# A hybrid residual block on one core: the second projection's product order, the place of its operand steps, and the start of the depthwise convolution's accumulators

## The chip, the cores and the metric

The kernel runs on one core of one Trainium2 chip. The metric is the device time of one execution in microseconds (us), the median over runs. The unchanged kernel was run three times; a fourth execution was recorded by the hardware profiler, and every row of the trace comes from that one.

## What is computed

One layer of a streaming encoder, on 1024 positions with 1024 channels. Two mixers share one input projection, and their outputs are gated, added and projected again; a feed-forward part follows.

```
proj = h @ w_in                       # h = adaLN(rmsnorm(x), c)
b, c, v, v_c, gl_c, gates = split(proj)
y_a = (b * causal_dwconv3(c * v)) @ w_short_out
u   = causal_dwconv31(v_c * sigmoid(gl_c)) + conv_conf_b
y_b = silu(layer_norm(u)) @ w_conf_out
g_a, g_b = split(sigmoid(gates))
x = x + g1 * ((g_a * y_a + g_b * y_b) @ w_o)
x = x + g2 * ((silu(h2 @ wa) * (h2 @ wb)) @ w_ffn_out)   # h2 = adaLN(rmsnorm(x), c)
return rmsnorm(x)
```

The shift, scale and gate vectors of adaLN (`sh1 ... g2`) come from `silu(c) @ w_ada + b_ada`, 48 blocks of 128 values.

## The kernel before

**Layout.** Channels lie on the 128 partitions, in 8 blocks; positions lie along the free dimension in two halves of 512. All matrix products are fp32 with both factors split into a high and a low part, so that a product of two 128x128 by 128x512 pieces takes three matmuls: high by high (L504), low activation by high weight (L505), high activation by low weight (L507). ScalarE (ACT) makes the high parts by a cast, of a weight at L243 (`wh`) and of an activation at L544 (for the second projection `z1h`, `z2h` and so on); VectorE (DVE) makes the low parts by a subtraction (L244, L545), for the weights of most of the input projection GpSimd (POOL).

**Seven products.** A pair of 1024x1024 weight quarters is multiplied by a scheme of the Strassen and Winograd kind: seven products, named "1" to "7", of 24 matmuls each (two output blocks `p`, four blocks `k` of 128 channels, three matmuls) in place of eight. Some products need sums of weight quarters and sums of activations first. `product` (L516) takes the next split weight from `next_w` (L465), which keeps the weights of the two following products in preparation (`AHEAD` = 2), and then issues the matmuls into PSUM banks `x`, `y`, `z`; `evac` takes the results out.

**The stages in order of time.** Start and norm; the input projection `w_duals` (some 100 to 560 us), beside which DVE runs the depthwise convolution of width 31; the first mixer's projection `w_short` ("ya"); the second mixer's projection `w_conf` ("yb", some 635 to 715 us), which this case calls the second projection; the output projection `w_o` ("mix"); the feed-forward part.

**Who orders the work.** The program text gives an order, and a scheduler lays out each engine's queue from it, at times in another order; each engine then takes its queue in the order laid out, and an instruction whose inputs are not there holds what stands behind it. `tc.issue_after(ins)` asks the scheduler to place the enclosed instructions behind `ins`.

**The second projection.** Two halves `d` of output channels have seven products each, 14 in all; `CONF_ORDER` (L120) and `yb_order` (L459) set their order, before 1(0) 1(1) 2(0) 2(1) 5(0) 5(1) 6(0) 6(1) 7(0) 7(1) 4(0) 4(1) 3(0) 3(1), where the bracket holds `d`. The weights come from `conf_units` (L384): SP loads a quarter (`get`, L390), and where a sum is needed POOL issues a second transfer that adds another quarter on the way (`add`, L397). Product 5 takes quarter 22 with 21 added; product 6 adds quarter 11 to that on DVE (L407, the tile `s2`); product 7 takes 21 with 11 added; product 3 adds quarter 12 onto product 6's own tile (L411), so this transfer waits until product 6's split has read the tile. `s2(0)` is `raw_5431` and `s2(1)` is `raw_5482` in the queues below. The activations' sums and splits for the coming products are called by `z_steps` (L1429) behind a product: `z_5`, `z_6`, `z_7`, `z_4` and `z_3`, each for four blocks `k`. `yb_evac` (L1376) copies a bank out on ACT (`vz`, L1395), or multiplies it by a gate on DVE and adds the result to `ma` by an adding transfer that POOL issues (L1388). The gates `gb` are loaded by POOL as well (`gates_b`, L1415), into six buffers that come free as those adding transfers land. So POOL's queue in this stage holds three kinds of transfers one behind the other: gate loads, adding transfers into `ma`, and adding transfers into weight tiles.

**The convolution.** `conv(j)` (L1143) runs once for each of 8 channel blocks. It works on even and odd positions apart, with two accumulators `a0` and `a1` in PSUM (the names `c0` and `c1` in the trace): 15 taps on the odd positions `od`, a sum, and 15 and 16 taps on differences (`diff`). A tap is one DVE instruction (L1158). The two accumulators are begun on ACT, `a0` with tap 1 and the bias (L1165), `a1` with tap 2 (L1166), and the odd taps go to `a0`, the even ones to `a1`. The results go to `cv` in DRAM and into running sums `tot` on POOL.

**The modulations.** In the input projection, seven pairs of product steps ("5" and "3" of `d` 3 to 9) each also compute one of the 48 adaLN blocks: a 128x1024 block of `w_ada` is loaded by SP into a free weight buffer, and DVE reduces it (L485). L1254 to L1256 do this after the product's call.

Of the kernel before, what the change touches and what calls it, by code (L numbers as in the profile page):

```python
# [37 lines left out]
AF = mybir.ActivationFunctionType  # L38
ALU = mybir.AluOpType
# [77 lines left out]
PRODUCTS = "1265734"  # L117


CONF_ORDER = "1256743"  # L120


MOD_FROM, MOD_AT = 16, "53"
# [15 lines left out]
def block_kernel(ctx: ExitStack, tc: tile.TileContext, x0, xT, c, vecs, ada, w_first, w_plain, w_duals,  # L139
# [69 lines left out]
    def col(base, k):  # L209
        return vec[:, base + k : base + k + 1]  # L210
# [245 lines left out]
    ya_order = [(d, m) for m in "12" for d in range(2)] + [(d, m) for d in range(2) for m in PRODUCTS[2:]]  # L456
    ya_units = [added_units([w_short[d, m] for m in range(4)]) for d in range(2)]
    plan += [ya_units[d][m] for d, m in ya_order]
    yb_order = [(d, m) for m in CONF_ORDER for d in range(2)]  # L459
    yb_units = [conf_units([w_conf[d, m] for m in range(4)], d) for d in range(2)]  # L460
    plan += [yb_units[d][m] for d, m in yb_order]
    plan += [(w_o[k], 1024) for ks in (range(KC), SECOND[KEPT:]) for k in ks]
# [680 lines left out]
    def conv(j):  # L1143
        eo = u[j].rearrange("p (n two) -> p n two", two=2)
        ev, od = eo[:, :, 0], eo[:, :, 1]
        diff = diffp.tile([P, T + CK - 1], F32, tag="diff", name="diff")
        d, e = diff[:, :NE], diff[:, NE : 2 * NE - 1]
        with tc.issue_after(read_at(conv_at(j))):
            nc.vector.tensor_tensor(d, ev, od, ALU.subtract)
            nc.vector.tensor_tensor(e, ev[:, 1:], od[:, : NE - 1], ALU.subtract)  # L1150
        a0, a1 = ps2_tile("c0"), ps2_tile("c1")
        n = 0

        def tap(out, src, s, wt, acc):
            nonlocal n
            n += 1
            with tc.issue_after(read_at(conv_at(j + n / TAPS))):
                tap.ins = nc.vector.scalar_tensor_tensor(  # L1158
                    out=out, in0=src[:, s : s + H], scalar=wt, in1=acc, op0=ALU.mult, op1=ALU.add
                ).ins  # L1160

        def both(s):
            return col(V_CW + 2 * s * KC, j) if s == CK // 2 else wsum[:, s * KC + j : s * KC + j + 1]

        nc.scalar.activation(a0, od[:, 1 : 1 + H], AF.Identity, bias=col(V_CB, j), scale=both(1))  # L1165
        nc.scalar.activation(a1, od[:, 2 : 2 + H], AF.Copy, scale=both(2))  # L1166
        for s in range(3, CK // 2 + 1):
            acc = a0 if s % 2 else a1
            tap(acc, od, s, both(s), acc)
        tap(od[:, :H], od, 0, both(0), a1)  # L1170
        with tc.issue_after(tap.ins):
            nc.vector.tensor_tensor(a0, a0, od[:, :H], ALU.add)
        for s in range(CK // 2):
            tap(eo[:, :H, 1] if s == CK // 2 - 1 else a1, e, s, col(V_CW + (2 * s + 1) * KC, j), a1 if s else a0)
        for s in range(CK // 2 + 1):
            tap(eo[:, :H, 0] if s == CK // 2 else a0, d, s, col(V_CW + 2 * s * KC, j), a0)
# [54 lines left out]
    for d, m in win_order:  # L1231
# [8 lines left out]
        if d + 1 < BEGUN and m == PRODUCTS[-1]:  # L1240
            for p in range(2):
                nc.scalar.copy(win_banks[d + 1]["x", p], m1[2 * (d + 1) + p])
        with tc.issue_after(mm3.ins) if (d, m) == (0, "6") else ExitStack():
            product(win_banks[d], m, th[m], win_evacs[d], onto="2")
        if (d, m) == win_order[0]:
# [5 lines left out]
                nc.gpsimd.memset(tot[h], 0.0)  # L1251
        if win_order.index((d, m)) >= len(win_order) - 7:
            q_steps.pop(0)()
        if m in MOD_AT and BEGUN < d < GATED:  # L1254
            modulation_of(MOD_FROM + n_mod, load(ada[MOD_FROM + n_mod], home=dual_units.home))
            n_mod += 1  # L1256
    while late:
        late.pop(0)()
# [167 lines left out]
    def z_3(k):  # L1426
# [2 lines left out]
    z_steps = {  # L1429
        (0, "1"): each(z_first, 4, 5), (1, "1"): each(z_first, 6, 7),  # L1430
        (0, "2"): each(z_5, 0, 1), (1, "2"): each(z_5, 2, 3), (0, "5"): each(z_6, 0, 1), (1, "5"): each(z_6, 2, 3),
        (0, "6"): each(z_7, *range(KH)), (1, "6"): each(z_4, *range(KH)), (1, "7"): each(z_3, *range(KH)),
        (0, "4"): lambda: [mg_split(j, 0) for j in range(0, KC, 2)],
    }
    for d, m in yb_order:
# [554 lines left out]
```

## Time and profile before

| | |
|---|---|
| median of 3 runs | 1456.21 us (1456.04 to 1456.32) |
| the profiled execution's own time | 1457.19 us |
| span of its trace | 1455.4 us |
| mean granted clock of TensorE | 0.995 |
| busy, share of the span | PE 99%, PE weight loads 81%, DVE 83%, ACT 45%, POOL 36% |
| DMA | 275.04 MB, mean 189 GB/s |

The span is what the trace covers from first to last instruction; the execution's own time is 1.8 us longer, for what lies around it. All times in the trace count from the span's start. PE is TensorE, SP the engine that issues most loads. In a row of the timeline stand the start, the length, the engine, the line and operation, output and inputs with their shape, the count of merged instructions, and in square brackets how long the engine had been idle before and what ended that. The matmuls' ends are modelled, and a matmul of 0.39 us stands next to the following one at a distance of 0.227 us, since they overlap.

### The profile page before, as it was taken

To read this page: it belongs to the slowest core of one execution; us is meant where nothing else is said; L and a number is where in the kernel's file an instruction comes from. 1 tells how busy PE (TensorE), PEld (TensorE's weight loads), DVE (VectorE), ACT (ScalarE), POOL (GpSimd) and SP (SyncE) were. 2 spreads that over 40 slices of the span, in tenths; PEclk is the share of its full clock that TensorE was granted. 3 is DMA by queue.
4 is the path that set the end of the run, shared out by engine and by line. 5 is a ranking of instruction groups with operands and counts; after the bars stand their busy time and mean duration, and the time that the engine had idled before them with its cause. 6 is when DMAs were issued, how large, how long until landed. Compare 5 with 4: busy or idle time off the path is not lost.

```text
span 1455.4 us, 17728 instructions
## 1 busy us (share of the span) xinstructions
PE 1434.4 (99%) x6322; PEld 1177.1 (81%) x6322; DVE 1204.0 (83%) x1657; ACT 656.6 (45%) x963; POOL 522.2 (36%) x496
## 2 busy tenths in 40 slices
PE   8999999999999999998999999999999999999997
PEld 4888888788878888887888888888888888888887
DVE  7996999999998998988988798877777665866676
ACT  4873433333333456566535464444444443322235
POOL 0016787677766661012222001101111115653405
PEclk9999999999999999999999999999999999999999
DMA  9743223333335569867795437645555449995903
GB/s 344 282 159 95 65 97 121 102 116 102 131 130 180 162 214 322 219 198 180 200 342 170 142 103 261 212 162 166 170 176 177 141 141 361 391 384 173 352 0 116
DMA packets 95946, 275.04 MB, mean 189 GB/s; under 512 B 10945, under 2 KB 12993, under 8 KB 95858
## 3 DMA queue, kind: packets, MB, share of 16 engines
q1 hardware_dynamic: 46672, 148.92, 30.1%
q0 software_dynamic: 44000, 111.36, 25.5%
q10 hardware_dynamic: 5186, 13.64, 2.4%
q8 instruction: 49, 0.80, 0.2%
q14 instruction: 39, 0.32, 0.1%
HBM read 203.09 MB, written 67.63 MB: 186 GB/s over the span
## 4 chain that ended last, share of the span: by engine, by line
PE 51%; POOL 1%; issue 0%; DVE 0%; POOLq 0%
PE x L507 8%; PE x L505 8%; PE x L504 8%; PE z L505 4%; PE z L507 4%; PE z L504 4%; PE y L504 2%; PE y L507 2%; PE y L505 2%; PE mix L504 2%; PE mix L507 2%; PE mix L505 2%; POOL x L1873 1%; PE bank L505 1%; PE bank L504 1%; PE bank L507 1%
## 5 line engine op out<-in xcount | busy, mean ns | idle before, releaser
L243 ACT CAST wh<-raw 128x1024 fp32r<-128x1024 f32 (+2 forms) x254 | 262.8, 1036 | 384.1 <-PE bank L505 137.6
L244 DVE TENSOR_TENSOR wl<-raw,wh 128x1024 fp32r<-128x1024 f32 (+2 forms) x176 | 211.7, 1204 | 42.1 <-ACT wh L243 40.2
L244 POOL TENSOR_TENSOR wl<-raw,wh 128x1024 fp32r<-128x1024 f32 x78 | 195.8, 2513 | 108.5 <-ACT wh L243 108.5
L1158 DVE SCALAR_TENSOR_TENSOR c<-diff,vec,c 128x512 f32<-128x512 f32 x232 | 165.0, 748 | 1.4
L1628 POOL DMA_DIRECT2D hid<-stage x70 | 37.4, 535 | 343.9 <-DVE stage L553 322.1
L504 PE MATMUL bank<-th,wh 128*128 128x512 f32 x336 | 132.1, 393 | 3.0 <-DVE sc L857 3.0
L505 PE MATMUL bank<-tl,wh 128*128 128x512 f32 x336 | 131.8, 392 | 0.0
L507 PE MATMUL bank<-th,wl 128*128 128x512 f32 x336 | 131.7, 392 | 0.0
L504 PEld LDWEIGHTS bank<-th,wh 128*128 128x128 f32 x336 | 63.7, 190 | 16.7 <-DVE sc L857 3.4
L505 PEld LDWEIGHTS bank<-tl,wh 128*128 128x128 f32 x336 | 63.8, 190 | 13.4
L507 PEld LDWEIGHTS bank<-th,wl 128*128 128x128 f32 x336 | 63.8, 190 | 13.3
L552 ACT CAST stage<-g 128x512 fp32r<-128x512 f32 x60 | 37.3, 621 | 76.9 <-DMA hid<-stage 41.0
L1158 DVE SCALAR_TENSOR_TENSOR c<-u,wsum,c 128x512 f32<-128x512 f32 x96 | 70.0, 747 | 0.8 <-ACT c L1166 0.2
L505 PE MATMUL x<-tl,wh 128*128 128x512 f32 x176 | 68.5, 389 | 0.0
L504 PE MATMUL x<-th,wh 128*128 128x512 f32 x176 | 68.5, 389 | 0.0
L507 PE MATMUL x<-th,wl 128*128 128x512 f32 x176 | 68.4, 390 | 0.0
L553 DVE TENSOR_TENSOR stage<-g,stage 128x512 fp32r<-128x512 f32 x60 | 41.2, 689 | 29.3 <-ACT stage L552 29.1
L1652 POOL DMA_DIRECT2D th<-hid x77 | 41.1, 534 | 51.4 <-PE x L507 33.9
L485 DVE CUSTOM_DVE_ANT_0 raw<-raw,cs,vec 128x1024 f32<-128x1024 f32 x24 | 40.1, 1670 | 12.3 <-DMA raw<-in_ada 12.3
L264 DVE TENSOR_TENSOR raw<-raw 128x1024 f32<-128x1024 f32 (+1 forms) x15 | 17.8, 1188 | 37.2 <-DMA raw<-in_w_fi 26.1
L1652 POOL DMA_DIRECT2D tl<-hid x77 | 41.2, 535 | 19.5 <-PE x L507 4.1
L504 PE MATMUL bank<-t2h,wh 128*128 128x512 f32 x112 | 43.6, 389 | 0.0
(830 smaller groups left out, 4149.4 us busy)
## 6 DMA issues: line engine op xcount, KB each, us to landing
hid<-stage POOLq DMA_DIRECT2D x70, 512.0 KB, 4.8
raw<-in_w_duals SPq DMA_DIRECT2D x65, 512.0 KB, 3.7
raw<-in_w_fi SPq DMA_DIRECT2D x54, 512.0 KB, 4.5
th<-hid POOLq DMA_DIRECT2D x77, 256.0 KB, 5.8
tl<-hid POOLq DMA_DIRECT2D x77, 256.0 KB, 5.9
ada<-in_ada SPq DMA_DIRECT2D x24, 512.0 KB, 7.1
raw<-in_ada SPq DMA_DIRECT2D x24, 512.0 KB, 3.6
raw<-in_w_fo SPq DMA_DIRECT2D x16, 512.0 KB, 6.1
```

The costliest lines, as they stand in the source:

```text
L243: hi = nc.scalar.copy(wh, raw)
L244: lo = lo_engine.tensor_tensor(wl, raw, f32(wh), ALU.subtract)
L264: eng.tensor_tensor(a["s1"], a["21"], a["22"], ALU.add)
L485: nc.vector.tensor_tensor_reduce(out=raw, in0=raw, in1=cs, scale=1.0, scalar=col(V_ADA, b), op0=ALU.mult, op1=ALU.add, accum_out=modc(b),)
L504: nc.tensor.matmul(ps, wh, xh, start=first, stop=False, skip_group_check=again)
L505: nc.tensor.matmul(ps, wh, xl, start=False, stop=False, skip_group_check=again)
L507: mm3.ins = nc.tensor.matmul(ps, wl, xh, start=False, stop=last, skip_group_check=again).ins
L552: t_split.act = nc.scalar.copy(hi, src).ins
L553: t_split.ins = nc.vector.tensor_tensor(lo, src, f32(hi), ALU.subtract).ins
L1158: tap.ins = nc.vector.scalar_tensor_tensor(out=out, in0=src[:, s : s + H], scalar=wt, in1=acc, op0=ALU.mult, op1=ALU.add).ins
L1628: nc.gpsimd.dma_start(hid_dram[key], s)
L1652: nc.gpsimd.dma_start(t, hid_dram[key][:, s])
```

## The change

Three edits.

**The order of the second projection.** `CONF_ORDER` now lists pairs: 1(0) 1(1) 2(0) 2(1) 5(0) 5(1) 6(0) 6(1) 3(0) 7(0) 7(1) 4(0) 4(1) 3(1). Product 3(0) has moved from the 13th place to the 9th. The operand steps follow: behind 6(0) now stand all of `z_3` (before `z_7`), behind 6(1) `z_7` (before `z_4`), and behind 3(0) `z_4` (before, `z_3` stood behind 7(1)). Since the weights are prepared two products ahead, the weight of 3(0) is now prepared while 6(0) is computed.

**The convolution.** `a0` is begun on DVE by a `tensor_scalar`; taps 2 to 5 all go to `a0`; `a1` is begun on ACT with tap 6, placed behind the last of these; taps 7 to 15 alternate as before. Each of the 8 convolutions has one instruction fewer on ACT and one more on DVE.

**The modulations.** The load of the `w_ada` block is now issued before the product's call, and the reduction is wrapped in `issue_after(mm3.ins)`, the last matmul of that product.

```diff
-CONF_ORDER = "1256743"
+CONF_ORDER = [(d, m) for m in "1256" for d in range(2)] + [(0, "3")] + [(d, m) for m in "74" for d in range(2)] + [(1, "3")]
...
-    yb_order = [(d, m) for m in CONF_ORDER for d in range(2)]
+    yb_order = CONF_ORDER
...
-        nc.scalar.activation(a0, od[:, 1 : 1 + H], AF.Identity, bias=col(V_CB, j), scale=both(1))
-        nc.scalar.activation(a1, od[:, 2 : 2 + H], AF.Copy, scale=both(2))
-        for s in range(3, CK // 2 + 1):
+        with tc.issue_after(read_at(conv_at(j))):
+            nc.vector.tensor_scalar(a0, od[:, 1 : 1 + H], both(1), col(V_CB, j), ALU.mult, ALU.add)
+        for s in (2, 3, 4, 5):
+            tap(a0, od, s, both(s), a0)
+        with tc.issue_after(tap.ins):
+            nc.scalar.activation(a1, od[:, 6 : 6 + H], AF.Copy, scale=both(6))
+        for s in range(7, CK // 2 + 1):
             acc = a0 if s % 2 else a1
             tap(acc, od, s, both(s), acc)
...
+        mod_raw = load(ada[MOD_FROM + n_mod], home=dual_units.home) if m in MOD_AT and BEGUN < d < GATED else None
         with tc.issue_after(mm3.ins) if (d, m) == (0, "6") else ExitStack():
             product(win_banks[d], m, th[m], win_evacs[d], onto="2")
...
-        if m in MOD_AT and BEGUN < d < GATED:
-            modulation_of(MOD_FROM + n_mod, load(ada[MOD_FROM + n_mod], home=dual_units.home))
+        if mod_raw is not None:
+            with tc.issue_after(mm3.ins):
+                modulation_of(MOD_FROM + n_mod, mod_raw)
             n_mod += 1
...
-        (0, "6"): each(z_7, *range(KH)), (1, "6"): each(z_4, *range(KH)), (1, "7"): each(z_3, *range(KH)),
+        (0, "6"): each(z_3, *range(KH)), (1, "6"): each(z_7, *range(KH)), (0, "3"): each(z_4, *range(KH)),
```

What the scheduler makes of it is seen in the queues. A row there gives the line, the operation, the output and its inputs with their tile numbers, the shape, and in brackets the semaphores on which the instruction waits: `DMASW` stands for a transfer that POOL issued, `DMAHW` for one that SP issued, the other names for engines.

ACT's queue at the time of products 5(1) and 6(0), before. `wh_5536` is the high weight of product 7(0), made from `raw_5533`, which an adding transfer of POOL fills:

```order
L243 CAST wh_5485<-raw_5482 128x1024 [waits DVE_49,Activation_49]
L544 CAST z6h_5470<-t2z_5468 128x512 [waits DVE_49]
L1269 ACTIVATE cv7_4987<-cv7_4987,vec_95 128x512 [waits DVE_49]
L243 CAST wh_5536<-raw_5533 128x1024 [waits DMASW2_49,PE_49,Activation_49]
L544 CAST z6h_5478<-t2z_5476 128x512 [waits DVE_49]
L1395 COPY vz_5501<-y_5279 128x512
L1395 COPY vz_5515<-y_5280 128x512 [waits PE_49]
L544 CAST z6h_5521<-t2z_5519 128x512 [waits DVE_49]
L544 CAST z6h_5529<-t2z_5527 128x512 [waits DVE_49]
```

The same place now. `wh_5534` is the high weight of product 3(0), made from `raw_5431`, which is `s2(0)` with quarter 12 added:

```order
L243 CAST wh_5485<-raw_5482 128x1024 [waits DVE_49,Activation_49]
L544 CAST z6h_5470<-t2z_5468 128x512 [waits DVE_49]
L1275 ACTIVATE cv7_4987<-cv7_4987,vec_95 128x512 [waits DVE_49]
L243 CAST wh_5534<-raw_5431 128x1024 [waits DMASW3_49,PE_49,Activation_49]
L544 CAST z6h_5478<-t2z_5476 128x512 [waits DVE_49]
L1401 COPY vz_5501<-y_5279 128x512
L1401 COPY vz_5515<-y_5280 128x512 [waits PE_49]
L544 CAST z6h_5521<-t2z_5519 128x512 [waits DVE_49]
L544 CAST z6h_5529<-t2z_5527 128x512 [waits DVE_49]
```

One row has changed: between the first two blocks of product 6's activations that are cast here now stands the weight of 3(0), not that of 7(0), and it waits for another transfer of POOL. PE's queue, the same before and now, takes these blocks so (`bank_829` and `bank_830` belong to 6(0), `bank_831` to 6(1)):

```order
L504 MATMUL bank_829<-z6h_5470,wh_5434 128x512 [waits Activation_49]
L504 MATMUL bank_830<-z6h_5470,wh_5434 128x512
L505 MATMUL bank_829<-z6l_5471,wh_5434 128x512 [waits DVE_49]
L507 MATMUL bank_829<-z6h_5470,wl_5435 128x512
L505 MATMUL bank_830<-z6l_5471,wh_5434 128x512
L507 MATMUL bank_830<-z6h_5470,wl_5435 128x512
L504 MATMUL bank_831<-z6h_5470,wh_5485 128x512
L505 MATMUL bank_831<-z6l_5471,wh_5485 128x512
L504 MATMUL bank_829<-z6h_5478,wh_5434 128x512 [waits Activation_49]
```

Eight matmuls use the block `z6h_5470`; the ninth is the first that needs `z6h_5478`.

POOL's queue in the same stage, before. `raw_5431` and `raw_5588` are the weights of 3(0) and 7(1), `ma40` and `ma60` take the results of product 2(1):

```order
L397 DMA raw_5533<-in_w_conf 128x1024 [waits DMAHW1_49,DMASW2_49,DVE_49]
L1388 DMA ma00_4669<-gb_5325 128x512 [waits DMASW3_49,DVE_49]
L1388 DMA ma20_4683<-gb_5327 128x512 [waits DMASW4_49,DVE_49]
L1415 DMA gb_5645<-gate_b3_121 128x512 [waits DMASW5_49,DMASW3_49]
L1415 DMA gb_5683<-gate_b5_123 128x512 [waits DMASW6_49,DMASW4_49]
L1388 DMA ma40_4731<-gb_5378 128x512 [waits DMASW7_49,DVE_49]
L1388 DMA ma60_4745<-gb_5380 128x512 [waits DMASW0_49,DVE_49]
L1415 DMA gb_5685<-gate_b7_125 128x512 [waits DMASW7_49,DMASW1_49]
L1415 DMA gb_5739<-gate_b1_119 128x512 [waits DMASW2_49,DMASW0_49]
L397 DMA raw_5431<-in_w_conf 128x1024 [waits DVE_49]
L397 DMA raw_5588<-in_w_conf 128x1024 [waits DMAHW2_49]
```

And now; `raw_5582` and `raw_5641` are the weights of 7(0) and 7(1):

```order
L397 DMA raw_5582<-in_w_conf 128x1024 [waits DMAHW1_49,DMASW2_49,DVE_49]
L1394 DMA ma00_4669<-gb_5325 128x512 [waits DMASW3_49,DVE_49]
L1394 DMA ma20_4683<-gb_5327 128x512 [waits DMASW4_49,DVE_49]
L1421 DMA gb_5639<-gate_b2_120 128x512 [waits DMASW5_49,DMASW3_49]
L1421 DMA gb_5698<-gate_b1_119 128x512 [waits DMASW6_49,DMASW4_49]
L1394 DMA ma40_4731<-gb_5378 128x512 [waits DMASW7_49,DVE_49]
L1394 DMA ma60_4745<-gb_5380 128x512 [waits DMASW0_49,DVE_49]
L1421 DMA gb_5700<-gate_b3_121 128x512 [waits DMASW7_49,DMASW1_49]
L1421 DMA gb_5738<-gate_b5_123 128x512 [waits DMASW2_49,DMASW0_49]
L397 DMA raw_5431<-in_w_conf 128x1024 [waits DVE_49]
L397 DMA raw_5641<-in_w_conf 128x1024 [waits DMAHW2_49]
```

The gates are those of other products, but the kinds of transfers stand in the same order: the addition for 3(0) stands behind two gate loads, and these wait for the landing of `ma40` (`DMASW7`) and `ma60` (`DMASW0`).

ACT's queue in the convolution stage, in the fourth convolution, before:

```order
L952 ACTIVATE bank_830<-bank_830 128x512 [waits PE_49]
L922 COPY bank_827<-bank_831 128x512 [waits DVE_49,PE_49]
L1165 ACTIVATE c0_4256<-u3_1605,vec_95,wsum_109 128x512 [waits DVE_49]
L922 COPY bank_828<-bank_832 128x512 [waits PE_49]
L854 ACTIVATE bank_829<-p3_1834,vec_95 128x512
```

And now:

```order
L952 ACTIVATE bank_830<-bank_830 128x512 [waits PE_49]
L922 COPY bank_827<-bank_831 128x512 [waits DVE_49,PE_49]
L243 CAST wh_2064<-raw_1962 128x1024 [waits PE_49,Activation_49]
L922 COPY bank_828<-bank_832 128x512 [waits DVE_49,PE_49]
L854 ACTIVATE bank_829<-p3_1834,vec_95 128x512 [waits DVE_49]
```

The begin of the accumulator between the two copies of banks is gone from ACT, and a cast of a weight has come into its place. On DVE the two reductions of one `d` now stand close together in every `d`. Around the last pair (`raw_3115` and `raw_3187`, where `raw_2974` and `raw_3148` stood) the rows have the same sequence as before: reduction, two taps, four instructions of the short convolution (L857), a sum (L869), one L857, reduction, L857. The single reduction that stood alone behind it (of `raw_3229`) is gone, and one more now stands at the stage's begin.

## The prediction

> **What bounds the kernel now.** I read the page's busy times first, then PE's waits, then the queues at the two longest waits.
>
> ```profile
> PE 1434.4 (99%) x6322; PEld 1177.1 (81%) x6322; DVE 1204.0 (83%) x1657; ACT 656.6 (45%) x963; POOL 522.2 (36%) x496
> PE bank L504 <- ACT z7h L544: 3.7, 1, 3.7
> PE bank L504 <- DVE sc L857: 3.0, 1, 3.0
> ...
> PE bank L504 <- ACT bank L922: 1.1, 1, 1.1
> ```
>
> PE is busy 99% of the span, and the matmuls are the same before and after. So the time can change only at PE's gaps, at the clock behind a gap, and by new gaps. Three gaps lie where the change acts: 3.7 us in the second projection, 3.0 and 1.1 us in the input projection. The rows left out belong to the kernel's start, which is untouched. The gap in the second projection costs more than its length:
>
> ```profile
> 687.10 0.39 PE L504 MATMUL bank<-z7h,wh 128*128 128x512 f32 x1
> 691.19 0.50 PE L504 MATMUL bank<-z7h,wh 128*128 128x512 f32 x1 [3.70 <-ACT z7h L544]
> ...
> 691.10:695.60 4.50, 4.41 (x12) 3.13 (x13) 3.72 (x5) 4.03 (x8) 0.00 (x0) 0.62 0.54 137
> 695.60:700.00 4.40, 4.40 (x21) 3.64 (x20) 3.29 (x6) 2.33 (x4) 0.83 (x1) 1.00 0.32 111
> ```
>
> The first two rows are the timeline of PE; in the others stand the stretch, the busy time and count of PE, weight loads, DVE, ACT and POOL, then the granted clock. Behind the gap the clock is 0.62 for 4.5 us, so 1.7 us are lost there: this gap costs 3.7 + 1.7 = 5.4 us. Its cause is named `z7h`, but the timeline of ACT shows what held that cast:
>
> ```profile
> 675.33 1.05 ACT L243 CAST wh<-raw 128x1024 fp32r<-128x1024 f32 x1 [0.54 <-ACT cv L1269]
> 676.29 0.61 ACT L544 CAST z6h<-t2z 128x512 fp32r<-128x512 f32 x1
> ...
> 685.11 0.64 ACT L544 CAST z7h<-cv 128x512 fp32r<-128x512 f32 x1
> 689.57 1.04 ACT L243 CAST wh<-raw 128x1024 fp32r<-128x1024 f32 x1 [3.83 <-DMA raw<-in_w_conf]
> 690.52 0.61 ACT L544 CAST z7h<-cv 128x512 fp32r<-128x512 f32 x1
> ```
>
> The next block's `z7h` stood behind the cast of 7(1)'s weight, which waited 3.83 us for an adding transfer. From the start of that cast, which begins when the transfer has landed, to PE's resumption (691.19) passed 1.6 us. So a weight cast that waits for POOL's transfer stops PE if an activation cast that PE needs stands behind it.
>
> **The change part by part: the second projection.** At the place of the row at 675.33, where ACT cast 7(0)'s weight without waiting for it, now stands the cast of 3(0)'s weight, and behind it the `z6h` of the row at 676.29. When does 3(0)'s transfer land? One row of DVE, one of SP, then POOL's timeline and landing times:
>
> ```profile
> 670.05 1.22 DVE L244 TENSOR_TENSOR wl<-raw,wh 128x1024 fp32r<-128x1024 f32 x1
> ...
> 668.40 9.70 SPq L227 DMA_DIRECT2D raw<-in_w_conf  x3
> ...
> 668.47 1.85 POOL L1388 DMA_DIRECT2D ma<-gb  x2
> 676.32 0.57 POOL L1415 DMA_DIRECT2D gb<-gate_b  x1 [6.00 <-DMA ma<-gb]
> 677.96 0.56 POOL L1415 DMA_DIRECT2D gb<-gate_b  x1 [1.07 <-DMA ma<-gb]
> 678.51 1.84 POOL L397 DMA_DIRECT2D raw<-in_w_conf  x2
> ...
> DMA to landing us min/median/max: 7.3/8.0/8.6
> DMA to landing us min/median/max: 5.2/7.9/12.4
> DMA to landing us min/median/max: 8.1/8.1/8.1
> ```
>
> The landings are of the two `ma` transfers at 668.47, of all six adding transfers for weights, and of the first at 678.51. POOL stood at two gate loads until the `ma` transfers had landed, and issued 3(0)'s addition at 678.51, though its tile had been free since product 6(0)'s low part was made, at 670.05 + 1.22 = 671.3. Before, this had no price, since 3(0) came 13th. Now the same two waits stand ahead of it in POOL's queue, and the products 2(0) and 2(1) that they follow from are unmoved. So the issue stays at 678.5, and the landing lies between 678.5 + 5.2 = 683.7 and 678.5 + 8.1 = 686.6. I take 684.8, between the ends: the last of SP's three loads (issued near 678 before, for product 4(1)) now has to wait for 3(0)'s own tile, and leaves this stretch less crowded.
> ```profile
> 675.31 0.62 PE L504 MATMUL bank<-z6h,wh 128*128 128x512 f32 x2
> ...
> DMA to landing us min/median/max: 3.2/4.6/8.6
> ...
> L244 DVE TENSOR_TENSOR wl<-raw,wh 128x1024 fp32r<-128x1024 f32 (+2 forms) x176 | 211.7, 1204 | 42.1 <-ACT wh L243 40.2
> ```
>
> An outer bound: the second row is that of the adding transfers into `ma` from 655 to 700 us. If those two landed near the least and the middle of these, after 3.2 to 4.6 us, the gate loads would go at 673 to 674, 3(0)'s addition near 674.5, and it would land near 680.
>
> PE begins product 6 at 675.31. In the new queue eight matmuls use the block cast before that point, at 0.227 us each, so PE stops near 677.1. It resumes 1.6 us behind the landing: 684.8 + 1.6 = 686.4. The gap is 9.3 us (8.2 to 11.1; 4.5 for the outer bound). Behind it the clock falls as it did behind the gap of 3.7 us and of 3.0 us:
>
> ```profile
> 427.00:430.00 3.00, 0.02 (x1) 0.00 (x0) 3.00 (x4) 1.77 (x3) 2.84 (x2) 0.87 0.12 19
> 430.00:436.00 6.00, 5.99 (x14) 4.74 (x15) 5.83 (x10) 1.05 (x2) 1.62 (x2) 0.50 0.96 336
> 436.00:440.00 4.00, 4.00 (x18) 3.25 (x18) 4.00 (x5) 2.22 (x4) 2.30 (x1) 0.99 0.02 8
> ```
>
> At 430 the clock was 0.50 for about 5.7 us, so some 2.8 us were lost; at 691 it was 1.7 us. I take 2.2 us. The page "TensorE: Matmul & The Clock Gate" of the Trainium skill (Part 1) states that the clock is halved after an idle window of about 3.4 us and restored after about as much sustained work; by that the gap of 2.99 us alone need not have cost the clock, and a long gap would cost about 1.7 us (an estimate from that page), which would make the sum 0.5 us less. Here the trace differs on both counts: 2.99 us were enough, and the return took 5.7 us.
>
> The low part of the weight (DVE, 1.2 us) stands ahead of the low parts of the activations in DVE's queue, and the remaining casts come one by one behind the gap; I allow 1.5 us for small gaps there (1 to 2.5), an estimate from one weight split of 1.2 us and one cast of 0.61 us. The old gap at 691 goes with its 5.4 us: the cast of 7(1) now stands after 686.4 + the 40 matmuls left of 6(0) and 6(1), far behind its landing at 689.5. The sum for this edit: 9.3 + 2.2 + 1.5 - 5.4 = **+7.6 us**, from 8.2 + 1.7 + 1.0 - 5.4 = +5.5 to 11.1 + 2.8 + 2.5 - 5.4 = +11.0, and 4.5 + 2.8 + 1.5 - 5.4 = +3.4 for the outer bound. What comes late next is small: the addition for 3(0)'s results into `ma`, on which the gates of 4(0) wait, has several products of 5.4 us (24 times 0.227) before it is needed.
>
> **The convolution's begin.** One gap has its cause in the removed instruction:
>
> ```profile
> 259.70 0.57 ACT L922 COPY bank<-bank 128x512 f32<-128x512 f32 x1 [1.33 <-PE bank L507]
> 264.91 0.81 ACT L1165 ACTIVATE c<-u,vec,wsum 128x512 f32<-128x512 f32 x1 [4.64 <-DVE u L1158]
> 265.66 0.54 ACT L922 COPY bank<-bank 128x512 f32<-128x512 f32 x1
> 266.25 0.50 PE L504 MATMUL bank<-h40h,wh 128*128 128x512 f32 x1 [1.14 <-ACT bank L922]
> ```
>
> ACT stood 4.64 us at the begin of `a0`, waiting for the previous convolution, and the copy that product 2 needs stood behind it. That instruction leaves ACT, the copy follows its bank at once, and the gap of 1.14 us goes: **-1.1 us**. No cold clock followed it, so there is nothing more to gain.
>
> DVE gets one instruction more per convolution:
>
> ```profile
> L1158 DVE SCALAR_TENSOR_TENSOR c<-u,wsum,c 128x512 f32<-128x512 f32 x78 | 57.5, 747 | 0.8 <-ACT c L1166 0.2
> DVE raw L485 <- DMA raw<-in_ada: 11.0, 9, 2.2
> ```
>
> Eight times 0.747 is 6.0 us of work between 190 and 560 us, against 11.0 us in which DVE stood before reductions for their loads. I cost it at nothing, since the instructions that PE needs mostly stand behind such a wait; without that cover it is at most 6.0 us.
>
> **The modulations and the gap of 3.0 us.** The rows of DVE and POOL in front of 430:
>
> ```profile
> 418.51 2.11 DVE L485 CUSTOM_DVE_ANT_0 raw<-raw,cs,vec 128x1024 f32<-128x1024 f32 x1 [1.41 <-DMA raw<-in_ada]
> 425.89 3.40 DVE L485 CUSTOM_DVE_ANT_0 raw<-raw,cs,vec 128x1024 f32<-128x1024 f32 x1
> 429.22 0.74 DVE L857 SCALAR_TENSOR_TENSOR sc<-p,vec,bank 128x512 f32<-128x512 f32 x1
> 425.83 2.37 POOL L244 TENSOR_TENSOR wl<-raw,wh 128x1024 fp32r<-128x1024 f32 x1 [6.30 <-ACT wh L243]
> ```
>
> A reduction that takes 3.40 us beside POOL's subtraction stands ahead of the L857 for which PE waits. The order that the change asks for binds nothing there: the last matmul of the product is long issued when DVE comes to the row, and DVE's sequence around both reductions is unchanged. Its load cannot come earlier either, since the weight buffer it goes into is read by POOL first. I cost this at 0; if the gap went whole, it would be 3.0 + 2.8 = 5.8 us less.
>
> **Sum.** +7.6 - 1.1 = +6.5 us: the profiled execution's 1457.2 becomes 1463.7, and since the median of the runs lies 1.0 us below it, I predict **1462.7 us**. My case's own range is +3.4 - 1.1 = +2.3 to +11.0 - 1.1 = +9.9, so 1458.5 to 1466.1.
>
> **Rivals.** *POOL is not held (other side).* If 3(0)'s addition were issued as soon as its tile is free (671.3), it would land by 671.3 + 5.2 = 676.5, and PE would resume at 678.1 in place of 677.1, a gap of 1.0 us too short for a cold clock, as at 266 (below 1.14); the old gap goes, so 1.0 - 5.4 - 1.1 = -5.5 us: 1450.7. The point from which it decides is a landing at 678.3: the gap is then 2.8 us, and 2.8 + 2.2 + 1.5 equal the 6.5 us that go. For it speaks that the tile is free early; against it that both gate loads stand ahead and their `ma` landings took over 7 us. Chance 0.09.
>
> *The 430 gap goes too.* If the shifted loads move the reduction away from POOL's subtraction, +6.5 - 5.8 = +0.7 us: 1456.9. For it speaks that the reduction takes 2.11 us elsewhere; against it the unchanged sequence. The page "SBUF — State Buffer" of the Trainium skill (SBUF: two separate sides) says that a VectorE instruction with two SBUF inputs and a GpSimd instruction shut each other out for whole instructions; the 3.40 us beside 2.37 us of POOL agree. Chance 0.12.
>
> *DVE falls behind in the convolution.* If the 6.0 us of added work are not covered, and about 4 us of them reach PE, +6.5 + 4 = +10.5 us: 1466.7. For it speaks 83% busy; against it the 11.0 us. Chance 0.13.
>
> **How the numbers follow.** My case has 0.66, the rivals 0.09, 0.12 and 0.13. A measurement of this kernel tells about 0.2% (2.9 us) from no change. Faster by more is the first rival: 0.09. Within 0.2% (1453.3 to 1459.1) are the second rival and a small part of my case's low end: 0.14. Slower is the rest: 0.77. The range that leaves out 2 in 10 reaches from the second rival to the third: 1457 to 1467.
>
> **What would show it.** In the new trace PE's longest wait should be for `z6h` (L544) near 677 to 687 us, with ACT idle for `raw<-in_w_conf` at L243 in front of it, and POOL's L397 at about 678.5. The wait for `z7h` and the wait for L922 at 266 should be gone, the wait for L857 at 430 still there. The prediction is wrong if the cast of 3(0)'s weight does not wait, or if the gap at 430 is gone.

## The result

The changed kernel takes 1469.23 us, the median of 4 runs (1467.35 to 1470.56); the unchanged one 1456.12 us in its 4 runs (1455.57 to 1456.32). The ratio is 1.009, with an interval of 1.0072 to 1.0107: 13 us slower, where 6.5 us were forecast and 1467 was the range's upper end.

The profiled execution of the changed kernel took 1469.08 us with a span of 1467.3 us, 11.9 us more than before. PE's waits on the changed kernel (in total, times, longest, us):

```profile
PE bank L504 <- DVE sc L857: 10.1, 4, 4.8
PE bank L504 <- ACT z6h L544: 8.4, 1, 8.4
```

The wait for `z6h` is the forecast one, and those for `z7h` and for L922 are gone. But the wait for L857 has become four. Where the time lies is read from three landmarks of PE, the first matmul of each named kind. The view of one tile gives them behind the durations, as "first to last start". Before:

```profile
L504 PE MATMUL begun<-h30h,wh x5: 389/389/389, 60.9 to 80.0; 128*128 128x512 f32 x5
L504 PE MATMUL bank<-z1h,wh x16: 389/389/389, 642.6 to 652.8; 128*128 128x512 f32 x16
L504 PE MATMUL mix<-mg00h,wh x8: 389/389/389, 724.9 to 762.9; 128*128 128x512 f32 x8
```

And of the changed kernel:

```profile
L504 PE MATMUL begun<-h30h,wh x5: 389/389/389, 60.1 to 79.2; 128*128 128x512 f32 x5
L504 PE MATMUL bank<-z1h,wh x16: 389/389/397, 648.6 to 658.8; 128*128 128x512 f32 x16
L504 PE MATMUL mix<-mg00h,wh x8: 389/389/389, 737.0 to 775.0; 128*128 128x512 f32 x8
```

I call the time from the first to the second landmark stage 1 (input projection and first mixer) and from the second to the third stage 2 (the second projection). Stage 1 grew from 581.7 to 588.5 us (+6.8), stage 2 from 82.3 to 88.4 us (+6.1). The start differs by -0.8 us and the rest by -0.2 us: 6.8 + 6.1 - 0.8 - 0.2 = 11.9 us. So stage 2 came out near its forecast of +7.6, and stage 1, forecast at -1.1, holds the miss.

**Stage 2 in the changed kernel.** The timelines of POOL (with the landing of its last row) and of ACT:

```profile
681.27 0.57 POOL L1421 DMA_DIRECT2D gb<-gate_b  x1 [5.17 <-DMA ma<-gb]
682.28 0.56 POOL L1421 DMA_DIRECT2D gb<-gate_b  x1 [0.44 <-DMA ma<-gb]
682.83 1.84 POOL L397 DMA_DIRECT2D raw<-in_w_conf  x2
...
DMA to landing us min/median/max: 7.0/7.0/7.0
```

```profile
689.97 1.04 ACT L243 CAST wh<-raw 128x1024 fp32r<-128x1024 f32 x1 [9.26 <-DMA raw<-in_w_conf]
690.92 0.61 ACT L544 CAST z6h<-t2z 128x512 fp32r<-128x512 f32 x1
```

POOL stands at the two gate loads until the `ma` transfers have landed, issues 3(0)'s addition at 682.83, and it lands 7.0 us later. ACT stands 9.26 us at the cast of that weight; the `z6h` for which PE waits comes behind it. And PE, in the timeline and in windows (stretch, busy time and count, granted clock, DMA):

```profile
681.24 0.62 PE L504 MATMUL bank<-z6h,wh 128*128 128x512 f32 x2
...
691.59 1.22 PE L504 MATMUL bank<-z6h,wh 128*128 128x512 f32 x2 [8.37 <-ACT z6h L544]
...
691.50:697.00 5.50, 5.42 (x14) 0.56 0.84 218
```

Product 6 begins at 681.24. Behind the gap the clock is 0.56 for 5.5 us, which loses 2.4 us (2.2 forecast).

**Stage 1 in the changed kernel.** DVE and PE at the first of the new waits, changed kernel:

```profile
268.92 2.60 DVE L485 CUSTOM_DVE_ANT_0 raw<-raw,cs,vec 128x1024 f32<-128x1024 f32 x1 [3.77 <-DMA raw<-in_ada]
272.10 1.40 DVE L857 SCALAR_TENSOR_TENSOR bank<-p,vec,bank 128x512 f32<-128x512 f32 x2
273.42 1.40 DVE L857 SCALAR_TENSOR_TENSOR sc<-p,vec,bank 128x512 f32<-128x512 f32 x2
274.21 0.50 PE L504 MATMUL bank<-th,wh 128*128 128x512 f32 x1 [1.74 <-DVE sc L857]
```

DVE at the same place before:

```profile
266.55 1.28 DVE L485 CUSTOM_DVE_ANT_0 raw<-raw,cs,vec 128x1024 f32<-128x1024 f32 x1 [1.01 <-DMA raw<-in_ada]
268.42 1.41 DVE L857 SCALAR_TENSOR_TENSOR bank<-p,vec,bank 128x512 f32<-128x512 f32 x2
```

A modulation's reduction stands ahead of the four L857 that free a bank for product 5, with one tap of the convolution between. Before it waited 1.01 us for its load and took 1.28 us, and the L857 came long before PE asked at 274.54. Now it waits 3.77 us, takes 2.60 us, and PE, which without the old gap at 266 would have asked at 272.5, waits 1.74 us. At 314 the reduction does not wait but is stretched beside a subtraction on POOL:

```profile
308.39 3.23 DVE L485 CUSTOM_DVE_ANT_0 raw<-raw,cs,vec 128x1024 f32<-128x1024 f32 x1
...
308.14 2.40 POOL L244 TENSOR_TENSOR wl<-raw,wh 128x1024 fp32r<-128x1024 f32 x1 [1.93 <-ACT wh L243]
```

3.23 us stand against 1.25 for the shortest reduction of that stage, and the difference of 2.0 us is more than the 1.74 us that PE waits there. At 437 both stand ahead of PE's wait, a late load at the pair's first reduction and a stretched second one:

```profile
426.71 1.29 DVE L485 CUSTOM_DVE_ANT_0 raw<-raw,cs,vec 128x1024 f32<-128x1024 f32 x1 [3.76 <-DMA raw<-in_ada]
433.26 3.37 DVE L485 CUSTOM_DVE_ANT_0 raw<-raw,cs,vec 128x1024 f32<-128x1024 f32 x1
...
433.20 2.35 POOL L244 TENSOR_TENSOR wl<-raw,wh 128x1024 fp32r<-128x1024 f32 x1 [7.89 <-ACT wh L243]
```

At 354 the reduction (at 349.08, 2.71 us) waits for no load. The four reductions that stand last ahead of the four waits each began while a subtraction on POOL was running, and each ended 1.08 or 1.09 us after that subtraction did: at 271.52 behind 270.43, at 311.62 behind 310.54, at 351.79 behind 350.70, at 436.63 behind 435.55. Against the 1.25 us of the shortest reduction, the stretch is what was left of POOL's instruction less some 0.2 us. The POOL rows of the first and the third:

```profile
268.02 2.41 POOL L244 TENSOR_TENSOR wl<-raw,wh 128x1024 fp32r<-128x1024 f32 x1 [1.20 <-ACT wh L243]
...
348.30 2.40 POOL L244 TENSOR_TENSOR wl<-raw,wh 128x1024 fp32r<-128x1024 f32 x1 [1.48 <-ACT wh L243]
```

### The profile page after: what moved, and what is told of

Read it like the earlier page. It is cut to its first block, busy times and chain, and to the rows that moved or that the text cites. A ratio compares the mean times of both kernels' runs of the same rounds, so it can differ in the third digit from the quotient of the medians.

```text
span 1467.3 us, 17736 instructions
## 1 busy us (share of the span) xinstructions
PE 1436.7 (98%) x6322; PEld 1177.6 (80%) x6322; DVE 1215.4 (83%) x1665; ACT 652.4 (44%) x955; POOL 522.6 (36%) x496
## 4 chain that ended last, share of the span: by engine, by line
PE 84%; DVE 6%; POOL 4%; issue 2%; DMA 2%; ACT 0%; POOLq 0%; DVEq 0%; ACTq 0%
PE bank L504 10%; PE bank L505 10%; PE bank L507 10%; PE x L507 8%; PE x L505 8%; PE x L504 8%; PE z L507 4%; PE z L505 4%; PE z L504 4%; PE y L505 2%; PE y L504 2%; PE y L507 2%; PE mix L505 2%; PE mix L504 2%; PE mix L507 2%
```

## The experiments

All stages below are read by the same landmarks, in one profiled execution per kernel, against the first trace of the unchanged kernel. That execution took 1457.19 us, longer than any other of the unchanged kernel on record (1450.4 to 1456.1 us beside the experiments), so a difference from its row can be too favourable to the other kernel by a few microseconds. Where it matters, PE's waits alone are given too. Some kernels have line numbers shifted by one to six.

| kernel | stage 1 | stage 2 |
|---|---|---|
| unchanged | 581.7 | 82.3 |
| changed | 588.5 | 88.4 |
| e1 second projection alone | 580.5 | 89.3 |
| e2 convolution alone | 580.3 | 81.1 |
| e3 modulations alone | 583.3 | 81.5 |
| e4 convolution and modulations | 586.9 | 81.1 |
| e5 as e4, reductions behind L857 | 580.1 | 81.4 |
| e6 as e3, reductions behind L857 | 576.3 | 80.6 |
| e7 as e1, gate loads behind 3(0)'s transfer | 580.5 | 85.0 |
| e8 unchanged, gate loads behind 7(1)'s transfer | 580.5 | 77.3 |
| e9 as e1, cast of 3(0) behind the z6h casts | 579.0 | 78.5 |
| e10 as e4, reductions of 128 columns | 574.9 | 80.5 |
| e11 e7 and e9 together | 578.9 | 77.0 |
| e12 e6 and e8 together | 576.9 | 77.3 |
| e13 as e4, additions into tot later | 585.2 | 81.8 |
| e14 e6 and e11 together | 577.1 | 77.0 |
| e15 changed kernel with e5's and e11's orders | 580.0 | 76.9 |

**One edit at a time: e1 to e4.** The edits are the three of the diff.

e1: 

> Only the second projection's order and steps are changed; convolution and modulations as before. The trace of the change shows two places of loss: about +6.7 us in the input projection and about +6.2 us in the second projection. Theory A (the second projection loses by itself, through the cast of 3(0)'s weight ahead of z6h): +6 us here, one wait of 8 to 9 us for z6h near 691, the 430 wait of 3.0 and the 266 wait of 1.1 still there. Rival B (the loss in the second projection comes from the input projection's delay, which shifts transfers): less than +2 us here.

e2: 

> Only the begin of the convolution's accumulators is changed. Theory A (the waits for the short convolution at 274, 314, 354 and 437 come from the moved modulations): -1 us, the wait at 266 gone and nothing new. Rival B (they come from the one DVE instruction more per convolution, 8 x 0.75 us, and the longer chain on one accumulator): +5 to +7 us, with the same four waits for L857 as in the changed kernel.

e3: 

> Only the modulations are changed (load before the product's call, reduction at the product's end). Theory A: +6 to +8 us, new waits of 1 to 2 us for L857 near 274, 314 and 354 and a longer one near 430. Rival B (the DVE instruction count of the convolution): 0 to +1 us.

e4: 

> Convolution and modulations changed, the second projection as before. Both theories: +6.7 us, the same waits for L857 as in the changed kernel, and the wait of 3.7 us for z7h near 691 as before. If it is less than the sum of the two single edits by over 1 us or more than it, the two edits act on one another.

Measured: e1 has its one wait for `z6h` (8.8 us) and stage 2 at +7.0 us, so the second projection loses by itself, as its theory A said. In stage 1 neither theory held. The convolution alone is 1.4 us shorter: a wait of 2.4 us came at 274, but the one near 430 went, since the scheduler there laid the second reduction behind the L857. The modulations alone are 1.6 us longer, with waits of 2.1 us at 311 and 5.1 us at 431. Together they are 5.2 us longer, with the four waits of the changed kernel: -1.4 and +1.6 do not add up to +5.2. PE's waits of stage 1 without the clock behind them, on which the slow clock of the first trace has no bearing, were 4.1 us in the unchanged kernel, 3.7 in e2, 7.2 in e3 and 9.9 in e4. So the single edits are -0.4 and +3.1 us, and together they are +5.8: the modulations lose by themselves, and 3.1 us come from the two together. The single runs say the same: e2, e3 and e4 took 0.4, 3.3 and 6.8 us more than the one run of the unchanged kernel beside them.

**What stands ahead of L857: e5, e6, e10.** e5 and e6 replace the order behind `mm3.ins`, an instruction of PE, with which the reductions still stood ahead of L857, by one on DVE:

```diff
-                nc.vector.scalar_tensor_tensor(
+                short_conv.ins = nc.vector.scalar_tensor_tensor(
...
-            with tc.issue_after(mm3.ins):
+            with tc.issue_after(short_conv.ins):
                 modulation_of(MOD_FROM + n_mod, mod_raw)
```

e5: 

> Convolution and modulations as in the changed kernel, the second projection as before; the reductions (L485) are ordered behind the last instruction of the short convolution (L857) on DVE. Theory A (PE's new waits come from a reduction standing on DVE directly in front of the four L857 that product 5 needs; it waits for its load or runs beside POOL's subtraction): all waits for L857 go, also the one near 430, and the input projection is some 12 us shorter than with both edits and no such order. Rival B (DVE has simply too much work in the stage): the waits stay, at other instructions of DVE, and less than 3 us are won.

e6: 

> As the run before, but the convolution as in the unchanged kernel. Theory A: the waits for L857 at 311 and 431 of the run with the modulations alone go; what stays is the wait of about 1 us for a bank copy at 266, if anything. Rival B: the same gain as from fewer instructions, none here, so waits at L857 remain.

All waits for L857 went in both, the one near 430 too. DVE in e6, at the place shown above:

```profile
264.05 1.41 DVE L857 SCALAR_TENSOR_TENSOR bank<-p,vec,bank 128x512 f32<-128x512 f32 x2
265.37 1.40 DVE L857 SCALAR_TENSOR_TENSOR sc<-p,vec,bank 128x512 f32<-128x512 f32 x2
...
267.30 3.20 DVE L485 CUSTOM_DVE_ANT_0 raw<-raw,cs,vec 128x1024 f32<-128x1024 f32 x1
```

The reduction still takes 3.20 us, now behind the L857 and at no price: stage 1 is 583.3 - 576.3 = 7.0 us shorter than in e3. So rival B falls as the cause of these waits. In e5 the gain over e4 is 6.8 us, not 12: with the convolution's edit a wait of 3.8 us came near 471, for L866 on DVE. e6, without that edit, has none there, so there the additional DVE work does reach PE.

e10 shortens the reductions and leaves part of the modulations out:

```diff
-            out=raw, in0=raw, in1=cs, scale=1.0, scalar=col(V_ADA, b),
+            out=raw[:, :w], in0=raw[:, :w], in1=cs[:, :w], scale=1.0, scalar=col(V_ADA, b),
...
-                modulation_of(MOD_FROM + n_mod, mod_raw)
+                modulation_of(MOD_FROM + n_mod, mod_raw, 128)
```

> Convolution and modulations as in the changed kernel, second projection as before; the 14 reductions of the input projection run over 128 of the 1024 columns, so that part of the modulations is left out (the loads stay whole). It parts the wait for a load from the length of a reduction (1.25 to 3.4 us). Theory A (both act at PE's waits: at 274 and 435 the load is late, at 314 and 354 the reduction is stretched by POOL's subtraction beside it): no wait for L857 at 314 and 354, a rest of under 2 us at 274 and under 3 us at 435. Rival B (only the late loads count): all four waits stay within 1 us.

All four waits went, the ones at 274 and 435 too, so the parting that it was made for failed: the reduction in front of 274 came at 265.08 instead of 268.66, since its load was issued at 261.35 instead of 264.15. It shows that the length of the reductions is part of the loop, not which share the load has.

**How the convolution reaches PE: e13.** The loads for the reductions wait for a buffer that POOL reads, and ahead of POOL's reads stand its additions into `tot`, which wait for a convolution's end. POOL there in the unchanged kernel, and POOL and PE in e2:

```profile
236.29 3.01 POOL L1185 TENSOR_TENSOR tot<-tot,u 128x512 f32<-128x512 f32 x2 [3.15 <-DVE u L1158]
```

```profile
237.37 3.02 POOL L1189 TENSOR_TENSOR tot<-tot,u 128x512 f32<-128x512 f32 x2 [5.78 <-DVE u L1158]
...
274.11 0.50 PE L504 MATMUL bank<-th,wh 128*128 128x512 f32 x1 [2.40 <-DVE sc L857]
```

Counted from the first landmark, the load in front of 274 is issued 202.1 us in before the change, 203.4 in e3, 204.6 in e2 and 204.7 in e4: most of the delay comes with the convolution's edit alone. e13 moves POOL's additions:

```diff
-        with tc.issue_after(lo):
+        with tc.issue_after(lo_at(conv_at(j + 1) + 0.7)[1]):
             for h in range(2):
                 nc.gpsimd.tensor_tensor(tot[h], tot[h], u[j][:, halves[h]], ALU.add)
```

> Convolution and modulations as in the changed kernel, second projection as before; POOL's additions into tot (L1185 in the unchanged kernel) are ordered later on POOL, behind about five more subtractions. Theory A (the longer convolution reaches PE through POOL: its end holds POOL's addition, this the subtractions, these the buffer for the modulation's load, and the reduction the L857): the load in front of 274 is issued 1.5 to 3 us earlier and the wait at 274 goes; the waits at 314 and 354 shrink or stay, since there DVE does not wait for the load. Rival B (the delay is on DVE alone): the wait at 274 stays at 1.7 us.

POOL and SP in e4, then in e13:

```profile
237.50 3.01 POOL L1189 TENSOR_TENSOR tot<-tot,u 128x512 f32<-128x512 f32 x2 [5.78 <-DVE u L1158]
...
264.15 0.33 SPq L227 DMA_DIRECT2D raw<-in_ada  x1
```

```profile
259.75 2.54 POOL L1189 TENSOR_TENSOR tot<-tot,u 128x512 f32<-128x512 f32 x2
...
259.81 6.28 SPq L227 DMA_DIRECT2D raw<-in_ada  x2
```

In e4 POOL stands 5.78 us at the addition; in e13 it has other work there, and the load is issued 4.3 us earlier. The waits at 274 and 314 go; the one at 354 stays at 1.7 us, and the one near 432 grows to 6.4 us. So theory A holds at 274. At 314 the wait goes on another way: in e13 the reduction there begins at 303.77, before POOL's subtraction (304.93), and takes 1.28 us, where in e4 it took 3.23:

```profile
303.77 1.28 DVE L485 CUSTOM_DVE_ANT_0 raw<-raw,cs,vec 128x1024 f32<-128x1024 f32 x1
...
304.93 2.41 POOL L244 TENSOR_TENSOR wl<-raw,wh 128x1024 fp32r<-128x1024 f32 x1 [3.03 <-ACT wh L243]
```

Why the last grows was not tried.

**The second projection: e7, e8, e9, e11.** e7 and e8 move gate loads on POOL (here e7; e8 names 7(1)'s transfer in the unchanged order):

```diff
-            nc.gpsimd.dma_start(raw, mat[b], accum_op=ALU.add)
+            conf_adds[d, b] = nc.gpsimd.dma_start(raw, mat[b], accum_op=ALU.add).ins
...
-        gates_b(d, m)
+        with tc.issue_after(conf_adds[0, "12"]) if yb_order.index((d, m)) >= 9 else ExitStack():
+            gates_b(d, m)
```

e9 moves the cast on ACT; e11 has both:

```diff
                 raw = add(a["s2"], "12")
+                return split_w(raw, 1024, (split.act,) if d == 0 else ())
```

e7: 

> Only the second projection is changed, with the gate loads of products 7(0) and later ordered on POOL behind the adding transfer of 3(0)'s weight. Theory A (3(0)'s transfer is late because POOL stands at gate loads ahead of it): the transfer is issued near 672 instead of 678.5 and lands by 677 to 680; the wait for z6h falls from 8.8 us to 0 to 3 us, and the second projection is 5 to 9 us shorter than with the new order alone. Rival B (the transfers are limited by bandwidth, not by the queue): the landing stays within 2 us and so does the wait.

e8: 

> The unchanged kernel with the gate loads of product 7(1) and later ordered on POOL behind the adding transfer of 7(1)'s weight. Theory A: that transfer is issued near 674.5 instead of 679 and lands by 684; the wait of 3.7 us for z7h and the half clock behind it go, 4 to 6 us less. Rival B (bandwidth): under 1.5 us less.

e9: 

> Only the second projection is changed, and the cast of 3(0)'s weight (L243) is ordered on ACT behind the last z6h cast; POOL's queue is as in the new order alone. Theory A (the cost is that cast's place on ACT, ahead of casts that PE needs first; the transfer itself is early enough for product 3(0)): the wait for z6h goes, no wait over 1.5 us takes its place, and the second projection is about 12 us shorter than with the new order alone, about 5 us shorter than in the unchanged kernel. Rival B (3(0)'s weight is late for its own product in any order): a wait of 4 us or more stands at the begin of 3(0).

e11: 

> Only the second projection is changed, with both the cast of 3(0)'s weight behind the z6h casts on ACT and the gate loads of 7(0) and later behind 3(0)'s transfer on POOL. Theory A: as with the late cast alone, within 1 us, since the transfer is then no longer what PE waits for. Rival B (the transfer bounds the stage): 2 us or more below the late cast alone.

In e7 the transfer is issued at 668.33, 6.1 us earlier than in e1 (674.46), but it then takes 8.6 us to land instead of 6.8, so it lands 4.3 us earlier, the wait falls from 8.8 to 4.6 us and the stage by 4.3 us. That is less than theory A expected (a wait of 0 to 3 us): POOL's queue is about half of the wait, and the transfer itself, now 1.8 us slower, is the rest. In e8 the wait for `z7h` is gone and the stage 5.0 us shorter, as forecast. Against the other traces with the old order, whose waits for `z7h` were 2.2 to 3.5 us (e2 to e6, e10, e13), it is 3.2 to 4.5 us shorter, and e8's one run took only 1.2 us less than the one unchanged run beside it; so the size is less sure than the cause. In e9 POOL is left alone, and only the cast stands elsewhere; ACT and the largest wait of PE in that stage:

```profile
676.79 0.62 ACT L545 CAST z6h<-t2z 128x512 fp32r<-128x512 f32 x1 [1.79 <-DVE t2z L558]
679.64 1.05 ACT L243 CAST wh<-raw 128x1024 fp32r<-128x1024 f32 x1 [2.22 <-DMA raw<-in_w_conf]
...
PE bank L506 <- DVE z3l L546: 1.1, 1, 1.1
```

The cast still waits for its transfer, but nothing that PE needs just then stands behind it: the stage falls from 89.3 to 78.5 us, 10.8 us (12 were expected). The whole price of the new order was the place of one cast. With both orders (e11) it is 77.0 us, between the two expectations and equal to e8's 77.3 in the old order within a third of a microsecond: by these two traces the order of the products is worth nothing by itself.

**Together: e12, e14, e15.** These have 3 rounds; the unchanged kernel's median beside them was 1452.6 us.

e12: 

> The unchanged convolution and the unchanged order of the second projection, with the reductions ordered behind the short convolution on DVE, and the gate loads of 7(1) and later behind 7(1)'s transfer on POOL. The single edits took about 5.4 us and 5 us off the two stages. Theory A (the gains lie at different waits and add up): 9 to 11 us below the unchanged kernel, near 0.993 of its time. Rival B (one undoes the other): under 6 us.

e14: 

> The unchanged convolution; reductions behind the short convolution on DVE; the new order of the second projection with the cast of 3(0)'s weight behind the z6h casts and the gate loads behind 3(0)'s transfer. Theory A (the order itself is neutral once the two queues are mended): within 1.5 us of the best kernel so far, which keeps the old order (1446.2 us). Rival B (the new order is worth something by itself): 2 us or more below it.

e15: 

> The changed kernel with all three of its edits, and with three orders added: reductions behind the short convolution on DVE, the cast of 3(0)'s weight behind the z6h casts on ACT, gate loads behind 3(0)'s transfer on POOL. Theory A (the loss is these three places in the queues): 1447 to 1450 us, 20 us below the changed kernel, with a rest at the wait for L866 near 473 that the convolution's edit brought. Rival B (the edits themselves cost time): above 1456 us.

e12: 1446.19 us, ratio 0.9954 (0.9937 to 0.9970), 6.4 us less. By the landmarks the two gains add up (4.8 and 5.0 us against the first trace of the unchanged kernel), but the unchanged runs beside e12 were themselves faster than that trace (median 1452.6 us against 1457.19), probably in part for the reason in the last section; by the runs the gain lies between the two expectations. e14: 1445.36 us, ratio 0.9952 (0.9938 to 0.9966), within 1 us of e12, as theory A said. e15: 1449.25 us, ratio 0.9977 (0.9968 to 0.9986): the changed kernel with three orders added is 3.4 us faster than the unchanged one, and against its own 1.009 that is 1.1%, some 16 us. Its largest wait in the two stages:

```profile
PE bank L506 <- DVE sig L868: 3.2, 1, 3.2
```

That is the rest which the convolution's edit brought (3.8 us in e5). In e14, without that edit, the waits for L868 are 1.9 us in all, and it is faster.

## Why the prediction was right and wrong

**The second projection: right.** The cast of 3(0)'s weight held the `z6h` behind it, as the steps said. The gap was forecast at 9.3 us and is 8.4 us; POOL's two gate loads did stand ahead; from the issue to the landing it took 7.0 us, where 6.3 were taken. The issue came 1.6 us behind the begin of product 6, where 678.5 - 675.3 = 3.2 us were taken; that these two errors partly cancel is luck, the mechanism is not. The half clock cost 2.4 us for 2.2. The sum of +7.6 stands against +6.1 in the changed kernel, +7.0 in e1, and +7.3 from e4 to the changed kernel, which differ in this edit alone.

**The gap at 266: right.** It is gone in e2, e4 and the changed kernel; the place where PE asks next came earlier by it. The removed instruction is not the only way: the gap is gone in e3 too, where `a0` still begins on ACT.

**The convolution on DVE, costed at nothing: wrong.** Here and in the next step the prediction failed: it took both edits' cost on DVE as nothing and so stage 1 at -1.1 us, and stage 1 measured +6.8 (+5.2 in e4). It said that the instructions which PE needs "mostly stand behind such a wait", and took the 11.0 us of DVE's waits before reductions as cover for 6.0 us of work. They were no cover. A wait that stands ahead of what PE needs does not absorb a delay when its own end is delayed too: the buffers for the loads on which DVE waited come free through POOL, POOL waits at `tot` for the end of a convolution, and that end came later. e2 shows a wait of 2.4 us at 274 from this edit alone, and e13 shows the path there. That e2 as a whole is not longer is luck: the scheduler's new layout took the wait near 430 away.

**The modulations, costed at nothing: wrong.** The step looked at the last pair alone, where the sequence was indeed unchanged; even there the wait did not stay at 3.0 us but grew to 5.1 in e3 and 4.8 in the changed kernel. In the earlier `d` the pair moved closer together and into other company on POOL; e3 has a new wait of 2.1 us at 311. PE's waits of stage 1 are 3.1 us longer from this edit alone. That the order asked for does not hold the reductions back was right, and e5 and e6 show what an order that binds would have done.

**The rivals.** The first did not come, since POOL stood at the gate loads, and e7, where it did not, shows that its gap of 1.0 us was too small: the landing took 8.6 us where 5.2 were taken, and the gap was 4.6 us. The second did not come either: the wait near 430 grew. The third, DVE falling behind, gave the nearest number (1466.7) with the wrong mechanism: e5 and e6 show the waits for L857 going with no less work on DVE, and only the wait for L866 in e5 and e15 is of the kind that it meant. With its 4 us, stage 1 would be at +2.9; it measured +6.8. No case of the prediction had the two edits act on each other. Of the waits at 354 and 437 (1.8 and 4.8 us) the stretch of the reductions can be 1.5 and 2.1 us, against the 1.25 us of the shortest one; how much of the rest at 437 is the late load stays open.

## What to carry to other kernels

Before a step is costed, read what stands behind it in each in-order queue: here the price of a whole reordering was one weight cast ahead of three activation casts, and the price of two small edits was a reduction ahead of four short instructions. Idle time of an engine is cover only if the thing that ends it does not move; follow that releaser back one or two queues, or take the wait as the engine's own lateness. An order behind an instruction of another engine did not hold the reductions back here, while an order that names the right predecessor on the same engine shortened a stage by 6.8 us (e5), 7.0 us (e6) and 10.8 us (e9).

## What the runs showed of the hardware

The same gap of 3.0 us on PE, in front of 430, does not always cost the clock. In six executions with the same wait there (unchanged, e1, e7, e8, e9, e11), stage 1 took 581.7, 580.5, 580.5, 580.5, 579.0 and 578.9 us. The windows behind the gap, first in e1, then in e11 (busy, count, granted clock, DMA):

```profile
428.00:434.00 6.00, 5.92 (x19) 0.72 0.94 332
```

```profile
428.00:434.00 6.00, 5.90 (x26) 1.00 0.95 330
```

In the first trace of the unchanged kernel the clock was 0.50 over this stretch, here it is 0.72 and 1.00: a gap of this length loses 0 to 2.8 us, differently from execution to execution. A shorter gap can do so too: behind the one of 1.78 us at 354 the clock was 1.00 in e4 and 0.72 over 6 us in the changed kernel, a loss of 1.7 us, which is the 1.6 us by which its stage 1 is longer than e4's. The changed kernel's window, then e4's:

```profile
354.40:360.40 6.00, 5.92 (x19) 0.72 0.58 215
```

```profile
353.80:359.80 6.00, 5.95 (x26) 1.00 0.60 218
```

The unchanged kernel's executions lie between 1450.4 and 1457.2 us; those with a mean granted clock of 0.995 took 1454.1 us or more, those with 0.997 or 0.998 took 1452.6 us or less. How much of that is these gaps is not shown. The Trainium skill's page "TensorE: Matmul & The Clock Gate" (Part 1) says that the window in which the clock is decided runs freely, so that the same kernel sees a different number of slow matmuls from run to run; the three windows at 430 agree. A gain that is read off one execution can be off by that much wherever a gap of about 2 us or more stands in the kernel. And an adding transfer that was issued earlier did not land earlier by as much: 3(0)'s took 6.8 us in e1 and 8.6 us when it was issued 6.1 us earlier in e7. These are two executions, and what slowed it was not tried.

How long a reduction on DVE takes is set by what POOL is doing when it begins. Of the 28 reductions beside the input projection in the unchanged and the changed kernel, 22 began while an instruction of POOL was running, and each of them ended 1.07 to 1.09 us after that instruction did (so 425.89 + 3.40 = 429.29 behind 425.83 + 2.37 = 428.20 at the old wait near 430); the other six took 1.25 to 1.29 us. A small shift in time can so make the same instruction 2 us longer or shorter.
